# The last columns of v among the first products of the RWKV scan, and the gate's matmuls spread through each step

## The chip, the cores and the metric

The kernel runs on one core of a Trainium2 chip. The metric is the device time of one execution in microseconds (us). Of the kernel before there are three such times and one profiled execution. The engines are TensorE (PE in the profile, with its weight loads as PEld), VectorE (DVE), ScalarE (ACT), GpSimd (POOL), and SyncE (SP), whose queue issues most of the transfers.

## The reference, cut to what matters

Two layers over 1024 tokens of width 1024; the change is in the second, an RWKV-7 layer with a SiLU gate (16 heads of 64):

```python
def rwkv7_scan(r, w, k, v, kk, a):
    ...
    def step(state, inp):
        r_t, w_t, k_t, v_t, kk_t, a_t = inp
        sa = jnp.einsum('bhvk,bhk->bhv', state, -kk_t)
        state = (state * w_t[:, :, None, :]
                 + sa[..., None] * (kk_t * a_t)[:, :, None, :]
                 + v_t[..., None] * k_t[:, :, None, :])
        y_t = jnp.einsum('bhvk,bhk->bhv', state, r_t)
        return state, y_t

def odd_mixer(h, mu, w_r, w_k, w_v, w_g, w0, w1, w2, a0, a1, a2, k_k, k_a, r_k, lnx_w, lnx_b, w_o):
    ...
    xr, xw, xk, xv, xa, xg = [h + xx * mu[i] for i in range(6)]
    r = xr @ w_r
    k = xk @ w_k
    v = xv @ w_v
    g = xg @ w_g
    ...
    ys = rwkv7_scan(tm(rh), tm(wh), tm(kh), tm(vh), tm(kk), tm(ah)).transpose(1, 0, 2, 3)
    ...
    y = (y + bonus.reshape(B, S, D)).astype(h.dtype) * jax.nn.silu(g)
    return y @ w_o
```

The kernel doesn't run the scan token by token. It cuts the 1024 tokens into 16 chunks of 64 and works on them in 8 blocks of two chunks; within a chunk the recurrence becomes products of 64x64 matrices for each head, and a triangular matrix to invert for each head.

## The kernel before, in words

**Projections.** r, k, v and g are 1024x1024 projections. Each operand is split into a high and a low part, so a product takes three matmuls. `odd_layer` makes r, k and v in turn, 256 columns at a time (c = 0 to 3), and in two halves of the tokens (f = 0, 1: token blocks 0 to 3 and 4 to 7 of 128). For v, one 128-token group of 256 columns is 24 matmuls of 128x256; two groups share a PSUM tile, which `ev_v` evicts on ACT into a tile and stores to v_d in DRAM. The last piece of v (c = 3, f = 1) is 96 matmuls and ends right before the scan. The gate g isn't made in `odd_layer`: `Gate.pieces` makes it during the scan, 16 groups of 8 pieces, 3 matmuls of 128x512 in each piece (L943). After a group's last piece ACT evicts it through SiLU and stores it to sg_d.

**The scan.** Three strings of tokens set the order of all work of the scan: `SCAN_START`, `SCAN_STEP` (run six times, for blocks 0 to 5), `SCAN_END`. Each token calls a function of the same short name; every engine gets its instructions in that order, SP its transfers too. The tokens that matter here:
- `ld`: load A and BK of a chunk (0.5 MB each, L1001 and L1003); `uv`: load its v rows.
- `al` (`alphas`, 32 + 32 matmuls of 64x64 in the profile's count, L1043 and L1046): makes M and AK from A and BK; ACT evicts them. `sM` stores M of a block's two chunks to DRAM (MA, L1055, four transfers), `lM` loads it back in another layout (Nt, L1099).
- `ip`, `ia`, `ie`, `ib`: the inverse of the 32x32 diagonal blocks, on DVE, cut into rows that `ib` calls a few at a time; `ic` stores the result (XT, L1171) and `lX` loads it as X (L1179).
- `mx`, `ma` (L1197), `mb` (L1210): the remaining quarter of the inverse from X and M. `ma` is the first on PE to need X.
- `sc` (`scores`, L1030, one half of a chunk): needs A and BK; ACT evicts it to MY. `mA`, `mY`: POOL masks AK and MY.
- `dec` (`decayed`, L1062): POOL scales BK in place when al and sc have read it. `T` (`transposed`, L1072): PE transposes the scaled BK.
- `V` and `U` (L1225, L1250), `st` (L1275, the product for the next state, which DVE adds to it), `Y` (L1285), `W` (L1235 and, for the output of the chunk before, L1294): the recurrence proper. `keep`: POOL scales the state.
- `g` with a number: that many gate pieces; `L`, `wx`, `gl`, `gx`: load and split the gate's weights; `xl`: load the gate's x for the second token half.

In a step, U, st, Y and W work on the block's own chunks c and c+1; al, sc, dec, T and the start of the inverse work two blocks ahead, and ic, lX, mx, ma, mb one block ahead. The work around each step's X is thus: SP stores M (`sM`), loads A and BK, stores XT, loads Nt, loads X; PE goes on with U1 to W2 and gate pieces until ma.

All of SP's transfers go out in order: one that waits for its data holds those behind it.

Of the kernel before, what the change touches and what calls it, by code (L numbers as in the profile page):

```python
# [8 lines left out]
F32 = mybir.dt.float32  # L9
# [8 lines left out]
P = 128  # L18
KT = D // P
NB = S // P  # L20
CB = 256
# [28 lines left out]
EVEN_PLAN = (  # L50
    "q0 k0 h0 z2 h1 q1 h2 k1 h3 va0 s0 h4 u0 h5 z3 h6 z0 h7 va1 s1 u1 z1")
SCAN_START = (
# [4 lines left out]
SCAN_STEP = (  # L57
    "U0 al0 ib2 st0 al1 Y0 uv1 keep1 mA0 mA1 W1 sM0 sc0 ib3 ld6 U1 sc1 g1 mY0 mY1 ic0 st1 dec0 lM0 Y1 g1 W2 keep2 "
    "ip0 lX0 gx1 uv2 sc2 Yd0 T0 g1 sc3 ia0 ld7 mx0 ma0 dec1 ie0 g2 mb0 g2 T1 g2 ib3 gl2")
SCAN_END = (  # L60
# [82 lines left out]
def load_wm(g, w, c0):  # L143

    return wm(split_wm(g, [load_m(g, w, c0, i) for i in range(2)]))
# [576 lines left out]
def mixed(g, hT, i, fs, x):  # L722

    nc = g.nc
    xh, xl = x
    for f in fs:
        for kk in range(4):
            h = g.s4([P, 2, 512], F32R, "xh")
            l = g.s4([P, 2, 512], F32R, "xl")
            for j in range(2):  # L730
                k = 2 * kk + j
                t = g.s2([P, 512], F32, "xm")
                if j and i == 0:
                    nc.vector.tensor_scalar(t, hT[kk, f][:, j, 1:513], g.onemu[:, i, k:k + 1], None, op0=OP.mult)
                else:
                    nc.scalar.activation(t, hT[kk, f][:, j, 1:513], AF.Copy, scale=g.onemu[:, i, k:k + 1])  # L736
                nc.vector.scalar_tensor_tensor(t, hT[kk, f][:, j, 0:512], g.pr[:, i, k:k + 1], t,  # L737
                                               op0=OP.mult, op1=OP.add)
                nc.scalar.activation(h[:, j], t, AF.Copy)
                (nc.vector if j or not i else nc.gpsimd).tensor_tensor(l[:, j], t, h[:, j].bitcast(F32), OP.subtract)  # L740
            xh[kk, f], xl[kk, f] = h, l
# [89 lines left out]
            nc.sync.dma_start(g.BK_d[64:128, f * 8:(f + 1) * 8, p, 1 - j], BK[64:128, :, j])  # L831


def odd_layer(g, a, hT, wt, out):
    nc, tc = g.nc, g.tc
    st = ExitStack()
    pool = st.enter_context(tc.tile_pool(name="prep", bufs=1, reuse_waits="tile"))
    prep = Prep(g, a, pool)

    def store(dst, ps, func):  # L840
        t = g.s2([P, 512], F32, "rt")
        nc.scalar.activation(t, ps, func)
        nc.sync.dma_start(dst, t)

    def ev_r(c):
        return lambda m, f, ps: store(g.r_d[2 * c + m][:, f * 512:(f + 1) * 512], ps, AF.Copy)

    def ev_k(c):
        return lambda m, f, ps: prep(2 * c + m, f, ps)

    def ev_v(c):
        def fn(b2, ps):
            t = g.s2([P, 2, 2, CB // 2], F32, "rt")
            for j in range(2):
                nc.scalar.activation(t[:, j].rearrange("p e (q d) -> p e q d", d=CH),
                                     ps[:, j].rearrange("p (q e d) -> p e q d", e=2, d=CH), AF.Copy)
                nc.sync.dma_start(g.v_d[(2 * b2 + j) * P:(2 * b2 + j + 1) * P, :, c * P:(c + 1) * P], t[:, j])
        return fn

    plan = []  # L860
    for i, n, fn, ld, ev in ((0, "rw_wr", chan_major, load_wm, ev_r), (2, "rw_wk", chan_major, load_wm, ev_k),
                             (3, "rw_wv", token_major, load_wk, ev_v)):
        for c in range(D // CB):
            plan.append((i, a[n][0], fn, ld, ev, c))
    w = load_wm(g, plan[0][1], 0)
    xn = ({}, {})
    mixed(g, hT, 0, (0,), xn)
    lora(g, hT, wt, prep.TH, prep.UA)
    mixed(g, hT, 0, (1,), xn)
    for j, (i, W, fn, ld, ev, c) in enumerate(plan):  # L870
        if c == 0:
            x, xn = xn, ({}, {})
        if j + 1 < len(plan):
            nxt = plan[j + 1][3](g, plan[j + 1][1], plan[j + 1][5] * CB)
        else:
            gate = Gate(g, a["rw_wg"][0], xn)
            gate.load(0)
            gate.load(1)
            gate.split(0)
            gate.split(1)  # L880
        if j == 9:
            norms(g)
        if j == XD:
            mixed_out(g, hT, 5, 1, g.xg_d)
        if c == 3:
            ni = plan[j + 1][0] if j + 1 < len(plan) else 5
            fn(g, x, w, ev(c), (0,))
            mixed(g, hT, ni, (0,), xn)
            fn(g, x, w, ev(c), (1,))
            if ni != 5:  # L890
                mixed(g, hT, ni, (1,), xn)
        else:
            fn(g, x, w, ev(c))
        w = nxt
    st.close()
    g.p2s.close()
    late = st.enter_context(tc.tile_pool(name="scan", bufs=1, reuse_waits="tile"))
    gate.pool = late
    g.s2 = lambda shape, dtype, name: late.tile(shape, dtype, name=name, bufs=1)
    rw = Rwkv(g, late)  # L900
    for c in range(2):
        rw.load(c)
    o = Out(g, a, out, late)
    with tc.manual_schedule(engines=ENG | {mybir.EngineType.SP}):
        rw.start(gate)
        for b in range(NB - 2):
            rw.step(b, gate)
    with tc.manual_schedule(engines=ENG | {mybir.EngineType.SP}):
        rw.end(gate, o)
    st.close()  # L910
# [67 lines left out]
class Rwkv:  # L978
# [326 lines left out]
    def start(self, gate):  # L1305
        g, nc = self.g, self.g.nc

        def zs(i):
            nc.gpsimd.memset(self.new_S(0), 0.0)

        self.pm = g.bB([P, 2, 2, 4, CH], "pm")
        ops = dict(L=gate.load, wx=gate.split, xl=gate.load_x, ld=self.load,
                   g=lambda i: [next(gate.rest, None) for _ in range(i)],
                   sc=lambda i: self.scores(i // 2, i % 2), al=self.alphas, sM=self.store_M, lM=self.load_M,
                   ip=self.inverse_p, ia=self.inverse_a, ie=self.inverse_d, ib=lambda i: [next(self.rows, None) for _ in range(i)],
                   ic=self.inverse_c, lX=self.load_X, mx=self.merge_x, ma=self.merge_a, mb=self.merge_b,
                   dec=self.decayed, T=self.transposed, mA=self.mask_AK, mY=self.mask_MY,
                   uv=self.load_uv, V=lambda i: list(self.Wkeys(i)), W=self.W, keep=self.keep, zs=zs)
        for name, i in order(SCAN_START):
            ops[name](i)  # L1320
# [244 lines left out]
```

## Time and profile before

| what | us |
|---|---|
| three runs | 1478.01, 1482.53, 1484.24 |
| median | 1482.53 |
| profiled execution | 1480.0 |
| its span | 1478.1 |
| PE busy in the span | 1308.3 (89%) |
| DVE, ACT, POOL busy | 897.8, 627.8, 548.4 |

The mean granted clock of PE over the span is 0.941. The span holds the work of one execution; the execution's own time is 1.9 us longer. The page of the profile gives busy time for each engine, the chain of work that ended last, and groups of instructions by line; the trace behind it can be cut into windows of time and listed by instruction. In rows of waits the numbers are the total in us, the number of waits, the longest. In a timeline row the first number is the start, the second the duration, and a bracket at the end gives the idle time before it and what ended that. In a row of windows the stretch is followed by its length, the busy time and number of instructions of each engine, PE's granted clock (1.00 is full speed), the share of DMA and GB/s.

### The profile page before, as it was taken

What the parts mean: (1) busy time and instruction counts of PE and PEld (TensorE: products, weight loads), DVE (VectorE), ACT (ScalarE), POOL (GpSimd) and SP (SyncE); (2) the same over time, 40 slices, a digit from 0 to 9 for tenths busy, and PEclk for the clock granted to TensorE, in tenths of its full rate; (3) what the DMA queues carried; (4) which work ended last, traced back from release to release, by engine and by line L of the source; (5) the groups of instructions that cost most, each with busy time, mean ns of one, the idle gap of its engine ahead of it and who ended that gap; (6) DMA issues with size and microseconds to landing.
All of it is one profiled execution on the core that took longest, in us unless ns stands there. A gap on an engine that the chain in (4) does not pass through costs nothing.

```text
span 1478.1 us, 30910 instructions
## 1 busy us (share of the span) xinstructions
PE 1308.3 (89%) x12773; PEld 1108.9 (75%) x12773; DVE 897.8 (61%) x1489; ACT 627.8 (42%) x1188; POOL 548.4 (37%) x353
## 2 busy tenths in 40 slices
PE   5899999899997999999997868998978788887877
PEld 5887788778896799978864436896767666667877
DVE  8741535663557426771599888512856677768884
ACT  4421535552454323552545554323434344454322
POOL 8750102030112612221343353203644444387751
PEclk9999999899999999999999979998978898979998
DMA  6377435350443334224177547517586666676412
GB/s 221 86 259 196 114 128 158 83 131 15 137 121 101 124 119 143 74 74 140 43 220 203 125 103 204 143 48 207 142 244 162 154 168 167 187 212 228 143 36 93
DMA packets 253275, 209.15 MB, mean 141 GB/s; under 512 B 79648, under 2 KB 215424, under 8 KB 253136
## 3 DMA queue, kind: packets, MB, share of 16 engines
q1 hardware_dynamic: 249536, 198.27, 47.1%
q10 hardware_dynamic: 3600, 8.91, 1.8%
q8 instruction: 100, 1.64, 0.5%
q14 instruction: 39, 0.32, 0.1%
HBM read 135.71 MB, written 71.43 MB: 140 GB/s over the span
## 4 chain that ended last, share of the span: by engine, by line
PE 53%; DVE 17%; DMA 9%; issue 8%; ACT 6%; POOL 4%; SPq 2%; ACTq 0%; DVEq 0%; POOLq 0%
PE pj L153 33%; PE pj L943 4%; PE pt L572 2%; PE pj L1477 2%; DMA kl<-dk 1%; DMA BK<-BK_d 1%; DMA w<-in_rw_a_dram 1%; DMA XT<-xm 1%; PE sp L562 1%; PE sp L559 1%; PE op L580 1%; DMA X<-XT 1%; ACT wh L105 1%; PE py L1285 1%; DVE xm L737 1%
## 5 line engine op out<-in xcount | busy, mean ns | idle before, releaser
L106 POOL TENSOR_TENSOR wl<-wraw,wh 128x1024 fp32r<-128x1024 f32 x38 | 93.6, 2466 | 168.6 <-ACT wh L105 157.5
L106 DVE TENSOR_TENSOR wl<-wraw,wh 128x1024 fp32r<-128x1024 f32 x46 | 70.8, 1545 | 94.5 <-ACT wh L105 51.4
L153 PE MATMUL pj<-hh,wh 128*128 128x512 f32 x320 | 127.3, 398 | 0.0
L153 PE MATMUL pj<-hh,wl 128*128 128x512 f32 x320 | 126.6, 396 | 0.0
L153 PE MATMUL pj<-hl,wh 128*128 128x512 f32 x320 | 126.6, 396 | 0.0
L105 ACT ACTIVATE wh<-wraw 128x1024 fp32r<-128x1024 f32 x84 | 88.1, 1056 | 61.9 <-DMA wraw<-in_w_in_even_dram 25.1
L153 PE MATMUL pj<-xl,wh 128*128 128x512 f32 x256 | 102.3, 400 | 2.6 <-DVE xl L740 2.6
L153 PE MATMUL pj<-xh,wh 128*128 128x512 f32 x256 | 102.2, 401 | 2.4 <-ACT ks L789 2.4
L153 PE MATMUL pj<-xh,wl 128*128 128x512 f32 x256 | 101.8, 398 | 0.2 <-POOL wl L106 0.2
L566 DVE CUSTOM_DVE_ANT_0 sc<-sp,tb 128x128 f32<-128x128 f32 (+3 forms) x64 | 48.2, 753 | 59.4 <-PE sp L562 50.8
L1477 PE MATMUL pj<-wh,yh 128*128 128x256 f32 x256 | 75.4, 294 | 5.1 <-DVE x L1481 3.9
L1477 PE MATMUL pj<-wh,yl 128*128 128x256 f32 x256 | 74.4, 291 | 4.6 <-POOL yl L106 4.5
L153 PE MATMUL pj<-wh,hh 128*128 128x256 f32 x256 | 75.1, 296 | 3.2 <-ACT hh L265 2.9
L737 DVE SCALAR_TENSOR_TENSOR xm<-hT,pr,xm 128x512 f32<-128x512 f32 x56 | 50.0, 933 | 44.0 <-ACT xm L736 43.7
L153 PE MATMUL pj<-wh,hl 128*128 128x256 f32 x256 | 75.3, 295 | 1.2 <-DVE hl L266 1.2
L153 PE MATMUL pj<-wh,yl 128*128 128x256 f32 x256 | 73.7, 288 | 1.9 <-POOL yl L624 1.9
L153 PE MATMUL pj<-wl,hh 128*128 128x256 f32 x256 | 74.6, 292 | 0.0
L153 PE MATMUL pj<-wh,yh 128*128 128x256 f32 x256 | 73.3, 286 | 0.8 <-ACT yh L623 0.8
L1477 PE MATMUL pj<-wl,yh 128*128 128x256 f32 x256 | 74.0, 289 | 0.0
L153 PE MATMUL pj<-wl,yh 128*128 128x256 f32 x256 | 72.9, 285 | 0.0
L153 PE MATMUL pj<-wh,xh 128*128 128x256 f32 x256 | 72.2, 282 | 0.6 <-ACT ks L789 0.5
L153 PE MATMUL pj<-wl,xh 128*128 128x256 f32 x256 | 72.2, 282 | 0.0
(320 smaller groups left out, 4062.3 us busy)
## 6 DMA issues: line engine op xcount, KB each, us to landing
wraw<-in_w_in_even_dram SPq DMA_DIRECT2D x28, 512.0 KB
tb<-tb SPq DMA_DIRECT2D x16, 512.0 KB
A_d<-AR SPq DMA_DIRECT2D x16, 512.0 KB
wraw<-in_rw_wg_dram SPq DMA_DIRECT2D x16, 512.0 KB
A<-A_d SPq DMA_DIRECT2D x16, 512.0 KB
BK<-BK_d SPq DMA_DIRECT2D x16, 512.0 KB
xt<-in_x_dram SPq DMA_DIRECT2D x8, 512.0 KB
dv<-vt SPq DMA_DIRECT2D x16, 256.0 KB
```

Source lines behind the costliest of these rows:

```text
L105: nc.scalar.activation(hi, raw, AF.Copy)
L106: sub.tensor_tensor(lo, raw, hi.bitcast(F32), OP.subtract)
L153: nc.tensor.matmul(ps, a(k), b(k), start=(n == 0), stop=(n == 3 * KT - 1))
L559: nc.tensor.matmul(sp[:, c0:c1], qs[:, b * P:(b + 1) * P], kh[:, c0:c1], start=True, stop=False)
L562: nc.tensor.matmul(sp[:, c0:c1], qs[:, b * P:(b + 1) * P], kl[:, c0:c1], start=False, stop=True)
L566: nc.vector.tensor_tensor_reduce(sc[:, :n], sp[:, :n], tb[:, off:off + n], 1.0, BIG, OP.add, OP.min, mn)
L572: nc.tensor.transpose(pt[:, j - j0, :], sc[:, j * P:(j + 1) * P], g.ident)
L580: nc.tensor.matmul(op[:, s0:QW], vt[:, j, :], pth[j // 4][:, j % 4, s0:QW], start=(j == 0), stop=False)
L737: nc.vector.scalar_tensor_tensor(t, hT[kk, f][:, j, 0:512], g.pr[:, i, k:k + 1], t, op0=OP.mult, op1=OP.add)
L943: nc.tensor.matmul(ps, u[:, k], v[:, k % 2], start=(k == 0 and i == 0), stop=(k == KT - 1 and i == 2))
L1285: nc.tensor.matmul(self.py[64 - 64 * e:128 - 64 * e, q], t["MY"][:, 8 * e + q], t["UV"][:, e, q], start=q == 0, stop=False)
L1477: nc.tensor.matmul(ps[:, i, :], u[:, k], v[:, k % 4], start=(k == 0 and j == 0), stop=(k == KT - 1 and j == 2))
```

## The change

Three things.

First, the last half of v's last columns is no longer made ahead of the scan. For the last projection `odd_layer` makes a generator, `last_values`, with the same 96 matmuls in 8 steps of 12 matmuls each, and the new token `vp` takes that many steps of it. `ev_v` takes its tile under the name XT, which the scan's pool shares with the gate's eviction.

Second, `SCAN_START` is ordered anew: al0 and al1 of the first block come behind 36 and 48 matmuls of the v half, with no gate piece ahead of them (15 before); the rest of v follows, then Nt's load, then the inverse and the gate pieces. Ahead of ma0 there are 32 gate pieces (58 before); the number of pieces in `SCAN_START` is the same, 64.

Third, `SCAN_STEP` has the same nine pieces, but six ahead of ma0 and three behind it (three and six before), each between two groups of the recurrence. al1 moves from between st0 and Y0 to behind W1, sc0 to behind Y1, sc1 with dec0 to behind W2, and T0 stands directly behind them. `SCAN_END` is unchanged.

```diff
 SCAN_START = (
-    "g4 L2 g4 L4 L3 g7 al0 al1 sM0 ip0 wx2 g2 sc0 L7 g2 sc1 dec0 L9 uv0 ld2 g3 wx3 sc2 g2 wx4 sc3 dec1 g2 lM0 T0 "
-    "ld3 L6 g4 mA0 mY0 ia0 L5 g2 al2 wx5 g2 sc4 T1 ld4 g3 al3 sM1 ie0 sc5 dec2 g3 wx6 ib8 sc6 g2 sc7 dec3 uv1 T2 "
-    "zs0 g3 ic0 g4 wx7 mA1 mY1 ip1 lM1 lX0 keep0 g4 T3 g5 L8 mx0 xl0 V0 uv2 ma0 g2 wx8 xl1 ia1 mA2 g2 xl2 mb0 ie1 "
-    "W0 ld5 mA3 g2 xl3 ib3")
+    "vp3 al0 vp1 al1 sM0 ip0 vp2 lM0 vp2 ia0 ie0 g4 L2 sc0 g4 L4 L3 sc1 dec0 ib8 ld2 g7 wx2 g2 sc2 L7 g2 sc3 dec1 "
+    "L9 uv0 T0 ld3 g3 wx3 ic0 ip1 lX0 g2 wx4 T1 al2 mA0 mY0 g2 L6 ld4 g4 sc4 L5 g2 wx5 mx0 al3 sM1 V0 uv2 ma0 sc5 "
+    "dec2 g2 mb0 T2 g3 lM1 sc6 g3 wx6 sc7 dec3 ia1 mA1 mY1 uv1 g2 zs0 g3 ie1 T3 g4 wx7 keep0 g4 mA2 g5 L8 xl0 g2 "
+    "wx8 xl1 g2 xl2 W0 ld5 mA3 g2 xl3 ib3")
 SCAN_STEP = (
-    "U0 al0 ib2 st0 al1 Y0 uv1 keep1 mA0 mA1 W1 sM0 sc0 ib3 ld6 U1 sc1 g1 mY0 mY1 ic0 st1 dec0 lM0 Y1 g1 W2 keep2 "
-    "ip0 lX0 gx1 uv2 sc2 Yd0 T0 g1 sc3 ia0 ld7 mx0 ma0 dec1 ie0 g2 mb0 g2 T1 g2 ib3 gl2")
+    "U0 al0 g1 ib2 st0 Y0 uv1 keep1 g1 W1 al1 mA0 mA1 sM0 ib3 ld6 U1 g1 gx1 g1 mY0 mY1 ic0 st1 lM0 Y1 sc0 g1 W2 "
+    "sc1 dec0 keep2 ip0 lX0 uv2 T0 Yd0 g1 sc2 sc3 ia0 ld7 mx0 ma0 dec1 ie0 g2 mb0 T1 g1 ib3 gl2")
...
+def last_values(g, x, w, evac):
+
+    wh, wl = w
+    for b in range(4, 8):
+        sl = slice((b % 4) * P, (b % 4 + 1) * P)
+        if b % 2 == 0:
+            ps = g.bA([P, 2, CB], "pj")
+        n = 0
+        for k in range(KT):
+            for i, v in ((0, wh), (0, wl), (1, wh)):
+                g.nc.tensor.matmul(ps[:, b % 2, :], x[i][k // 2, 1][:, k % 2, sl], v(k), start=(n == 0), stop=(n == 3 * KT - 1))
+                n += 1
+            if k == 3:
+                yield
+        if b % 2:
+            evac(b // 2, ps)
+        yield
...
     def ev_v(c):
         def fn(b2, ps):
-            t = g.s2([P, 2, 2, CB // 2], F32, "rt")
+            t = g.s2([P, 512], F32, "XT").rearrange("p (j e c) -> p j e c", j=2, e=2)
...
             mixed(g, hT, ni, (0,), xn)
-            fn(g, x, w, ev(c), (1,))
             if ni != 5:
+                fn(g, x, w, ev(c), (1,))
                 mixed(g, hT, ni, (1,), xn)
+            else:
+                gate.last = last_values(g, x, w, ev(c))
...
-        ops = dict(L=gate.load, wx=gate.split, xl=gate.load_x, ld=self.load,
+        ops = dict(vp=lambda i: [next(gate.last, None) for _ in range(i)], L=gate.load, wx=gate.split, xl=gate.load_x, ld=self.load,
```

The lines of the code below line 850 move down by 19 to 21 (L943 becomes L964, L1043 L1064, L1197 L1218).

On PE, at the scan's beginning, the matmuls of the gate (L943, tiles pj, xh, xl, wh, wl) that stood ahead of al0 (L1043 and L1046) before:

```order
L943 MATMUL pj<-xh,wh 128x512
L943 MATMUL pj<-xl,wh 128x512
L943 MATMUL pj<-xh,wl 128x512
L1043 MATMUL pt<-BK,A 64x64 x2
L1046 MATMUL pt<-A,BK 64x64 x2
```

The same place now, with v's last half (L844) ahead of al0 (L1064, L1067):

```order
L844 MATMUL pj<-wh,xh 128x256
L844 MATMUL pj<-wl,xh 128x256
L844 MATMUL pj<-wh,xl 128x256
L1064 MATMUL pt<-BK,A 64x64 x2
L1067 MATMUL pt<-A,BK 64x64 x2
```

al0 stood behind all of v and 45 gate matmuls; now it stands behind 36 of the 96 matmuls of v's last half.

On SP, at the same place, the order of transfers from the last stores of v (v_d) to the first load of Nt, before (wraw is the gate's weights):

```order
L857 DMA v_d<-rt 256x1x128 x18
L1001 DMA A<-A_d 128x1024 x2
L928 DMA wraw<-in_rw_wg_dram 128x8x128
L857 DMA v_d<-rt 256x1x128 x2
L928 DMA wraw<-in_rw_wg_dram 128x8x128 x2
L1003 DMA BK<-BK_d 128x1024 x2
L1055 DMA MA_129<-M 32x16x32 x4
L928 DMA wraw<-in_rw_wg_dram 128x8x128 x2
L1013 DMA UV<-v_d 64x512 x2
L1001 DMA A<-A_d 128x1024
L1003 DMA BK<-BK_d 128x1024
L1099 DMA Nt<-MA_129 64x1024 x2
```

And now:

```order
L876 DMA v_d<-XT 256x1x128 x16
L1022 DMA A<-A_d 128x1024 x2
L1024 DMA BK<-BK_d 128x1024 x2
L876 DMA v_d<-XT 256x1x128 x2
L1076 DMA MA_129<-M 32x16x32 x4
L1120 DMA Nt<-MA_129 64x1024 x2
L876 DMA v_d<-XT 256x1x128 x2
L949 DMA wraw<-in_rw_wg_dram 128x8x128 x3
```

BK's loads follow A's directly, and Nt's load follows the store of MA directly; the loads of the gate's weights and of the next chunks come behind both.

On PE, in a step, from the end of W2 (L1235, L1294) to ma (L1197), before:

```order
L1235 MATMUL ch<-S,A 64x64 x2
L1294 MATMUL py<-S,A 64x64 x2
L1030 MATMUL pm<-A,BK 64x64 x16
L1072 MATMUL pt<-ident,BK 128x128 x8
L943 MATMUL pj<-xh,wh 128x512
L943 MATMUL pj<-xl,wh 128x512
L943 MATMUL pj<-xh,wl 128x512
L1030 MATMUL pm<-A,BK 64x64 x16
L1197 MATMUL pt<-X,M 32x32 x32
```

And now (W2 L1256 and L1315, sc L1051, T0 L1093, the gate L964, ma L1218):

```order
L1256 MATMUL ch<-S,A 64x64 x2
L1315 MATMUL py<-S,A 64x64 x2
L1051 MATMUL pm<-A,BK 64x64 x16
L1093 MATMUL pt<-ident,BK 128x128 x8
L964 MATMUL pj<-xh,wh 128x512
L964 MATMUL pj<-xl,wh 128x512
L964 MATMUL pj<-xh,wl 128x512
L1051 MATMUL pm<-A,BK 64x64 x32
L1218 MATMUL pt<-X,M 32x32 x32
```

Here the first sc is sc2 before and sc1 now: T0 transposes BK after POOL's scaling, which waits for sc1; sc1 stood further up, behind U1, and stands now directly ahead of T0.

## The prediction

> **What bounds the kernel now.** I read the chain of work that ended last first, then windows cut at the borders of the scan (its beginning, its six steps, its end; the first window is the last half of v's projection), then what TensorE (PE) waits for in the steps.
>
> ```profile
> PE 53%; DVE 17%; DMA 9%; issue 8%; ACT 6%; POOL 4%; SPq 2%; ACTq 0%; DVEq 0%; POOLq 0%
> ```
>
> ```profile
> core 0: us, PE busy (x) PEld busy (x) DVE busy (x) ACT busy (x) POOL busy (x), PEclk, DMA share, GB/s
> 991.50:1003.10 11.60, 11.60 (x100) 11.60 (x99) 9.79 (x10) 9.86 (x19) 6.04 (x4) 1.00 0.14 38
> 1003.10:1088.90 85.80, 71.90 (x929) 56.20 (x927) 38.57 (x57) 29.54 (x47) 38.36 (x33) 0.88 0.72 202
> 1088.90:1127.30 38.40, 32.50 (x812) 27.38 (x811) 28.14 (x49) 15.33 (x27) 16.00 (x15) 0.78 0.73 207
> 1127.30:1160.50 33.20, 27.21 (x812) 22.88 (x811) 21.77 (x38) 15.00 (x27) 15.78 (x15) 0.90 0.65 167
> 1160.50:1192.40 31.90, 26.92 (x812) 22.83 (x811) 19.66 (x35) 15.29 (x27) 15.86 (x15) 0.95 0.60 150
> 1192.40:1225.70 33.30, 27.10 (x812) 22.39 (x811) 22.65 (x39) 14.73 (x26) 15.96 (x15) 0.95 0.68 170
> 1225.70:1259.80 34.10, 27.84 (x812) 23.29 (x811) 24.46 (x43) 14.74 (x26) 15.78 (x15) 0.90 0.65 166
> 1259.80:1292.70 32.90, 27.54 (x805) 22.54 (x804) 22.04 (x40) 13.63 (x24) 13.89 (x14) 0.90 0.66 171
> 1292.70:1478.10 185.40, 145.81 (x1671) 136.74 (x1670) 134.95 (x175) 69.58 (x146) 114.80 (x51) 0.88 0.43 143
> ```
>
> ```profile
> PE pt L1197 <- DMA X<-XT: 10.4, 7, 3.3
> PE pm L1030 <- issue: 6.7, 5, 2.7
> PE pt L1072 <- POOL BK L1062: 2.5, 3, 1.8
> PE pt L1043 <- DMA BK<-BK_d: 2.4, 1, 2.4
> ```
>
> PE is the largest part of the chain, but not all of it. The v half runs without a gap: 11.60 us for 96 matmuls of v and the first of the gate, some 0.12 us each. The scan's beginning leaves PE idle for 85.8 - 71.9 = 13.9 us, and each step for 5 to 6 us, both at a granted clock below 1. So time can be won in two ways: less idle PE, and fewer windows at half clock. In the steps the largest wait is that of ma (line 1197) for the transfer X, the next is the sequencer's own ("issue") ahead of sc (line 1030).
>
> **The beginning before.** The chain of waits over this stretch, and PE's and SP's timelines:
>
> ```profile
> 1003.14 5.58 PE pj L943 x24
> 1009.33 6.83 DMA BK<-BK_d
> 1021.07 0.61 ACT M L1047
> 1029.05 9.04 DMA Nt<-MA
> 1074.59 3.63 DMA X<-XT
> ```
>
> ```profile
> 1016.21 0.27 PE L1043 MATMUL pt<-BK,A 64*64 64x64 f32 x2 [2.64 <-DMA BK<-BK_d]
> ...
> 1076.18 0.28 PE L1197 MATMUL pt<-X,M 32*32 32x32 f32 x2 [6.32 <-DMA X<-XT]
> 1078.27 1.91 PE L1197 MATMUL pt<-X,M 32*32 32x32 f32 x62 [1.80 <-DMA X<-XT]
> ```
>
> ```profile
> 1021.69 1.96 SPq L1055 DMA_DIRECT2D MA<-M  x4
> ...
> 1028.55 1.09 SPq L1099 DMA_DIRECT2D Nt<-MA  x2
> ```
>
> ```profile
> 1038.10:1069.20 31.10, 30.68 (x392) 24.39 (x392) 29.91 (x34) 13.49 (x23) 22.48 (x15) 1.00 0.48 133
> 1083.70:1104.10 20.40, 17.35 (x553) 15.17 (x553) 18.74 (x36) 7.88 (x14) 6.31 (x6) 0.81 0.70 242
> ```
>
> One path: BK lands 1016.2, al0 and al1 make M, SP stores it (1021.69) and issues the load of Nt only 6.86 us later, behind six other loads; Nt lands 1038.1; DVE inverts (31.1 us); X lands 1078.27, 9.1 us after the inverse. PE fills that time with gate pieces and runs out: 6.32 + 1.80 = 8.1 us of waiting, then half clock (ma takes 1.91 us).
>
> **The change at the beginning.** In the chain 24 gate matmuls follow each other in 5.58 us, so a piece (three of them) takes 0.70 us in a run. al0 and al1 now come behind the first half of v and 36 of the last 96 matmuls of v, without a gate piece ahead of them.
> - BK: A and BK (two chunks, 2 MB) are now issued right behind the stores of v's first half, not at 1009.3. That half ends at 991.5, its stores some 2 us later; al0 needs 1.5 MB, 6 us at the 258 GB/s of the window 1184.6 to 1192.4 below: BK lands near 1000 (an estimate). PE finishes its 36 matmuls at 991.5 + 4.3 = 995.8 and waits about 4 us (2.6 before); then half clock, two al of 1.9 us (ma's ratio, 1.19 to 1.91, below) with 12 matmuls of v between: al1 done near 1006.5, 14.7 us before 1021.2.
> - Nt: SP has the load directly behind the store. M's eviction 0.6, store 2, landing some 3 us: Nt lands near 1015, against 1038.1, so 23 us earlier.
> - The inverse: 31.1 us in one place and 20.4 us in the other, where POOL is busy for 22.48 and 6.31 us beside it. POOL's splits and scalings lie beside it again, thinner; I take 25 (bounds 20.4 and 31.1): done 1040, X at 1040 + 9.1 = 1049.
> - PE until ma0: from 1006.5 the last 48 matmuls of v (5.6), 32 gate pieces (22.4), five sc (0.7 each, 3.5), two al (2.2), two T (2.1) and V0 (1.1) make 36.9: PE arrives at 1043.5 and waits 5.5 us (8.1 before), then about 3 us lost to half clock.
> - After ma0: ma 1.2, three sc 2.1, 32 pieces 22.4, mb 1.2, two T 2.1, W0 1.1, together 30.1, and 1.5 us of small waits: U0 at 1049 + 30.1 + 3 + 1.5 = 1083.6, against 1088.9. **Term: -5** us. With the inverse at 20.4 X comes with PE, and the half clock goes too: -12; at 31.1 X lands at 1055: +1.
>
> [...]
>
> **The change in a step.** Windows from Y0's end to X's landing and from X to the step's end, at half and at full clock; then PE's timeline (durations of what moves, ma after longer and shorter waits), SP's and POOL's:
>
> ```profile
> 1133.10:1150.40 17.30, 11.62 (x405) 9.60 (x403) 9.49 (x14) 7.63 (x14) 14.46 (x15) 0.97 0.68 157
> 1150.40:1160.50 10.10, 10.09 (x152) 8.18 (x152) 9.51 (x22) 4.01 (x7) 0.00 (x0) 0.71 0.89 255
> ...
> 1184.60:1192.40 7.80, 7.80 (x162) 6.35 (x154) 7.41 (x16) 4.64 (x8) 1.91 (x1) 1.00 0.93 258
> ```
>
> ```profile
> 1130.89 0.27 PE L1043 MATMUL pt<-BK,A 64*64 64x64 f32 x2
> ...
> 1132.00 1.15 PE L1285 MATMUL py<-UV,MY 128*64 128x64 f32 x32
> ...
> 1150.41 1.91 PE L1197 MATMUL pt<-X,M 32*32 32x32 f32 x62 [0.30 <-DMA X<-XT]
> ...
> 1170.89 0.69 PE L1030 MATMUL pm<-A,BK 64*64 64x64 f32 x32
> 1171.51 0.50 PE L943 MATMUL pj<-xh,wh 128*128 128x512 f32 x1
> ...
> 1172.40 0.69 PE L1275 MATMUL ch<-UV,BKT 128*64 128x64 f32 x16
> ...
> 1181.07 1.97 PE L1072 MATMUL pt<-ident,BK 128*128 128x128 f32 x8
> ...
> 1216.55 1.19 PE L1197 MATMUL pt<-X,M 32*32 32x32 f32 x62 [0.83 <-DMA X<-XT]
> ```
>
> ```profile
> 1135.07 2.17 SPq L1055 DMA_DIRECT2D MA<-M  x4
> ```
>
> ```profile
> 1142.20 1.91 POOL L1062 TENSOR_TENSOR BK<-BK,EC 128x1024 f32<-128x1024 f32 x1
> ```
>
> al1's matmuls run from 1130.89 to 1132.00 (1.1 us), Y0's 1.15; U, W, st and Y have as many and get 1.1 to 1.15 each. sc takes 0.69; a lone piece 0.9 (1171.51 to 1172.40), two 1.6; T half of the 1.97 at half clock, 1.0.
>
> X stands on SP behind the store of MA, the loads of A and BK, and Nt, so it lands a fixed time after MA's issue: 1150.41 - 1135.07 = 15.3 us in step 1. MA was issued 7.75 us after the step's start (1127.3). Now al1 comes behind W1: U0 1.15, al0 1.1, piece 0.9, st0 1.15, Y0 1.15, piece 0.9, W1 1.15, al1 1.1 make 8.6; with the eviction and SP's issue MA goes out at 9.35, **1.6 us later**, and X lands at 24.65 (9.35 + 15.3). PE reaches ma at: 8.6 + U1 1.15, two pieces 1.6, st1 1.15, Y1 1.15, sc0 0.7, piece 0.9, W2 1.15, sc1 0.7 = 17.1; T0 stands straight behind and waits for POOL's 1.91 us scaling (to about 19.2; 2.5 us in all steps together before); T0 1.0, piece 0.9, two sc 1.4: 22.5. So PE waits some 2.1 us at ma, and T0's wait is hidden under it. If X came earlier, T0's 2 us would stand open. The issue waits (6.7 us) fall into the same slack.
>
> Behind X stand three pieces fewer: 7.8 - 2.1 = 5.7 us at full clock, 10.1 - 2.1 = 8.0 at half. A step is 30.4 or 32.7, against a mean of 33.1 over steps 1 to 5. Which clock? A wait of 0.83 us left ma at 1.19; the longest X wait (3.3 in the list, step 1) was followed by a ma of 1.91, the longest issue wait ahead of sc (2.7) by the T of 1.97. 2.1 is nearer to the latter, so I take 31.8 between the two, a gain of 1.3. Bounds: -2.7 (full clock) and +0.8 (X as late in its step as in step 3, 1216.55 - 1192.4 = 24.15, plus 1.6, then 8.0: 33.8). **Term: five steps, -6.5** (-13.5 to +4).
>
> [...]
>
> Step 0 took 38.4 at clock 0.78 with a 2.4 us wait for BK (line 1043). That load is now issued with more lead; at 33.4, as the slower steps before, **-5** (0 if load and clock stay, -7 like the others). The end (185.4) is left alone: 0.
>
> **Sum.** 1480.0 (span 1478.1) - 5 - 5 - 6.5 = 1463.5; the median shown, 1482.53, lies 2.5 above that execution: **1466 us**.
>
> **Rivals.**
> - Slower: al1 now stands behind W1, and W1 reads the state that DVE adds between its rows of the inverse. Any wait there delays al1, MA and, through SP's order, X one for one. Price: a wait of 1.5 us gives 25.8 + 1.5 + 8.0 = 35.3, +2.2 in each of five steps, +11, and step 0 no faster; with -5 at the beginning 1488, with 0 there 1493: I give 1490. It decides from a wait of about 1 us. Against: the list above has no wait for DVE among the largest, and between st0 and W1 PE has Y0 and a piece, 2.05 us of cover, against al1 and Y0, 2.25, before. Chance 0.13.
> - Only the beginning gains (X binds the steps; BK's wait goes): -5 - 2.4: 1475. 0.17.
> - Only the steps gain, the inverse being long: +1 - 5 - 6.5: 1472. 0.14.
> - Full clock in the steps: a wait near 2 us, between the 0.83 that kept it and the 2.7 that lost it, is too short to lower it. -5 - 5 - 13.5: 1459; with a short inverse 1452. 0.18. [...]
> - The change doesn't do what it says: SP's queue is held by v's last stores, Nt lands no earlier in effect, waits change places: 1482. 0.06.
>
> The forecast has 0.32. **Range 1453 to 1488**: from the best of the beginning and steps nearly together (1480.0 + 2.5 - 12 - 5 - 13 = 1452.5) to the worst terms (+1, 0, +4: 1487.5). Half a per cent, 7.4 us, is about what a measurement of this kernel can tell from no change: the bound of "faster" is 1475.1. Faster 0.66: the forecast, the third and fourth rivals and half of the second, which stands on the bound, are 0.725, less 0.065 for sums of these that end above it; same 0.20: those two remainders and the last rival; slower 0.14: the first, and 0.01 of the last.
>
> **What would show it.** Right: al0 near 1000 after a wait of some 4 us; Nt landing before 1017; X of block 0 before 1052, with a wait under 6 us at ma0; no BK wait in step 0; MA issued 9 to 9.5 us after U0, X 24 to 25; T0 waiting 2 us in every step, steps of 31 to 32.5 us. Wrong: U0 after 1088, W1 waiting for DVE, steps over 33.1 us, or an end stage that differs from 185.4 by more than 2 us.

## The result, and the profile after

The change makes the kernel slower: 1497.33 us in the median of 6 runs (1490.38 to 1500.84), against 1479.83 in 6 runs of the kernel before, the three above among them. The medians differ by 17.5 us; the ratio on record is 1.0129, 95% interval 1.0099 to 1.0159, some 19 us, and the experiments below are compared by such ratios. The forecast was 1466, with a range of 1453 to 1488. The profiled execution took 1494.9 us (span 1492.8).

The stages of the changed kernel's profile, cut at the same places as those of before: v's first 36 matmuls of the last half (from the end of its first half at 988.4), the scan's beginning up to U0, the six steps, the end. The columns are as before.

```profile
988.40:992.80 4.40, 4.40 (x38) 4.23 (x36) 2.83 (x5) 4.13 (x8) 0.00 (x0) 1.00 0.47 93
992.80:1090.90 98.10, 77.61 (x993) 63.10 (x992) 42.05 (x67) 35.62 (x59) 43.88 (x36) 0.90 0.56 162
1090.90:1126.20 35.30, 26.65 (x812) 21.70 (x811) 21.03 (x38) 15.84 (x27) 16.01 (x15) 0.95 0.85 256
1126.20:1163.90 37.70, 28.55 (x813) 23.07 (x813) 27.91 (x44) 15.18 (x27) 16.70 (x15) 0.89 0.60 159
1163.90:1199.70 35.80, 29.95 (x814) 24.84 (x813) 23.30 (x39) 15.29 (x26) 16.47 (x15) 0.83 0.59 149
1199.70:1233.10 33.40, 26.90 (x816) 21.80 (x815) 19.23 (x35) 14.95 (x26) 16.20 (x15) 0.95 0.62 159
1233.10:1263.00 29.90, 24.89 (x812) 20.58 (x811) 21.25 (x38) 15.14 (x26) 16.88 (x15) 1.00 0.64 162
1263.00:1307.60 44.60, 32.47 (x804) 25.81 (x803) 26.05 (x45) 14.24 (x25) 14.01 (x14) 0.75 0.66 182
1307.60:1492.80 185.20, 142.24 (x1671) 133.81 (x1670) 133.27 (x175) 69.64 (x146) 114.76 (x51) 0.89 0.40 133
```

From the end of v's first half to U0 it takes 4.4 + 98.1 = 102.5 us; before it was 11.6 + 85.8 = 97.4. So the beginning lost 5.1 us where 5 were to be won. The six steps take 216.7 against 203.8, 12.9 more, and 11.7 of these stand in the last (44.6 against 32.9, at a clock of 0.75). The end is the same (185.2, 185.4). What PE waits for in the beginning (first fence) and in the steps (second):

```profile
PE pt L1218 <- ACT M L1068: 7.3, 1, 7.3
PE pt L1064 <- DMA BK<-BK_d: 4.3, 1, 4.3
PE ch L1246 <- POOL AK L1099: 3.3, 1, 3.3
```

```profile
PE pt L1093 <- POOL BK L1083: 13.8, 6, 2.7
PE pm L1051 <- ACT MY L1052: 6.7, 7, 2.4
PE pj L964 <- ACT wh L105: 5.6, 1, 5.6
PE ch L1246 <- issue: 3.2, 2, 1.9
```

X, the largest wait before, is in neither list. In its place stand waits for ACT and POOL: ma0 (L1218) 7.3 us for ACT, T (L1093) 2 us in each step for POOL's scaling, sc (L1051) for ACT's eviction, and one gate piece (L964) 5.6 us for the split of its weights. The waits put down to the sequencer ("issue") are as large as before in the steps, some 14 us together.

**The 7.3 us at ma0.** The timelines of PE, ACT, SP and DVE there:

```profile
1055.35 0.85 PE L1218 MATMUL pt<-X,M 32*32 32x32 f32 x24 [7.34 <-ACT M L1068]
```

```profile
1053.76 1.06 ACT L105 ACTIVATE wh<-wraw 128x1024 fp32r<-128x1024 f32 x1 [11.22 <-DMA wraw<-in_rw_wg_dram]
1054.72 0.58 ACT L1068 ACTIVATE M<-pt 128x512 f32<-128x512 f32 x1
1055.20 0.59 ACT L1069 ACTIVATE AK<-pt 128x512 f32<-128x512 f32 x1
```

```profile
1041.45 2.30 SPq L1200 DMA_DIRECT2D X<-XT  x4
...
1045.70 0.42 SPq L949 DMA_DIRECT2D wraw<-in_rw_wg_dram  x1
```

```profile
1013.61 0.42 DVE L1142 TENSOR_TENSOR DN<-Nt,rn 128x256 f32<-128x256 f32 x1 [11.44 <-DMA Nt<-MA]
...
1044.82 0.71 DVE L1206 STREAM_TRANSPOSE rt<-X 128x512 f32<-128x512 f32 x1 [7.01 <-DMA X<-XT]
```

X is there at 1044.82, when DVE reads it. ma0 starts at 1055.35, directly after ACT has evicted the M that the profile names. That M is al3's, of the next block: ACT stood 11.22 us before its split of a gate weight (wx5) that waited for the load, and M's eviction is behind it in ACT's order. The load (L5) was issued at 1045.70, behind X's on SP, which had waited 2.3 us for XT to land. al3 and ma0 take their PSUM from one pair of buffers in the code (`bC`, bufs=2), so ma0 can't start before al3's is evicted: that eviction ends at 1055.30. The data path of the forecast came in time; a weight load that it never counted didn't. PE itself came to ma0 at 1048.0 (1055.35 - 7.34), behind X and not ahead of it, since V0 had waited 3.3 us for POOL's mask of AK.

**The 5.6 us in the last step.** ACT and PE there:

```profile
1275.47 0.60 ACT L970 ACTIVATE XT<-pj 128x512 f32<-128x512 f32 x1
...
1279.24 0.33 ACTq L971 DMA_DIRECT2D sg_d<-XT  x1
1279.67 1.06 ACT L105 ACTIVATE wh<-wraw 128x1024 fp32r<-128x1024 f32 x1 [3.60 <-DMA XT<-xm]
```

```profile
1280.78 0.80 PE L964 MATMUL pj<-xh,wh 128*128 128x512 f32 x1 [5.61 <-ACT wh L105]
```

The piece needs the next weights at once: the group before ends with the piece ahead of `gx1`, and the split of the next weights stands directly between. Nine pieces a step against eight in a group move that border by one piece in each step; in the last it falls on gx1's new place. And ACT isn't free: the store of the finished group (sg_d) waits 3.6 us, with ACT behind it, for a transfer on SP, the inverse's store XT, on which its data doesn't depend. In the third and fifth steps the store holds ACT too, for 1.72 us (until X lands) and 2.25 us (until a load of A lands).

### The profile page after: what moved, and what is told of

It is laid out like the page before. It is cut to its first block, busy times and chain, and to the rows that moved or that the text cites. A ratio compares the mean times of both kernels' runs of the same rounds, so it can differ in the third digit from the quotient of the medians.

```text
span 1492.8 us, 30914 instructions
## 1 busy us (share of the span) xinstructions
PE 1298.1 (87%) x12773; PEld 1097.4 (74%) x12773; DVE 888.6 (60%) x1489; ACT 630.5 (42%) x1188; POOL 554.0 (37%) x353
## 4 chain that ended last, share of the span: by engine, by line
PE 51%; DVE 15%; DMA 9%; issue 8%; POOL 8%; ACT 7%; SPq 2%; ACTq 0%; DVEq 0%; POOLq 0%
PE pj L153 31%; PE pj L964 4%; POOL MY L1105 2%; PE pj L1498 2%; PE pj L711 1%; PE pt L572 1%; DMA wraw<-in_w_in_even_dram 1%; DMA BK<-BK_d 1%; PE pt L1093 1%; PE op L580 1%; ACT wh L105 1%; PE sp L559 1%; POOL BK L1083 1%; PE sp L562 1%; POOL wl L106 1%
## 5 line engine op out<-in xcount | busy, mean ns | idle before, releaser
L106 POOL TENSOR_TENSOR wl<-wraw,wh 128x1024 fp32r<-128x1024 f32 x38 | 94.3, 2483 | 161.3 <-ACT wh L105 148.5
L106 DVE TENSOR_TENSOR wl<-wraw,wh 128x1024 fp32r<-128x1024 f32 x46 | 72.7, 1587 | 95.5 <-ACT wh L105 50.1
L575 DVE TENSOR_TENSOR ptl<-pt,pth 128x512 fp32r<-128x512 f32 (+2 forms) x96 | 52.3, 553 | 29.8 <-ACT pth L574 16.7
L153 PEld LDWEIGHTS pj<-hh,wl 128*128 128x128 f32 x320 | 60.1, 188 | 13.3
```

The costliest lines, as they stand in the source:

```text
L106: sub.tensor_tensor(lo, raw, hi.bitcast(F32), OP.subtract)
L153: nc.tensor.matmul(ps, a(k), b(k), start=(n == 0), stop=(n == 3 * KT - 1))
L575: nc.vector.tensor_tensor(ptl[j0 // 4][:, 0:j1 - j0, i * P:(i + 1) * P], pt[:, :j1 - j0, :], o.bitcast(F32), OP.subtract)
```

## The experiments

Ratios are to runs of the kernel before, with 95% intervals. A step's or an end's length is that of the one profiled execution.

**The two halves of the change.** First the old step with the new beginning, then the new step with the old beginning.

```diff
-SCAN_STEP = (new)
+SCAN_STEP = (as before)
```

> The changed kernel with the old SCAN_STEP: only v's last columns and the order of the scan's beginning are changed. In the profile of the change the beginning (from v's first half to U0) is 5.1 us longer than before and the six steps 12.9 us. If the two parts add up, this kernel is some 5 us slower than before (about 1485). Rival: the beginning's loss comes out of what the new steps ask of it; then it gains the 5 us that the prediction gave it (about 1475).

1.0092 (1.0064 to 1.012): some 14 us slower, neither of the two numbers expected. The profile has the same wait at ma0 (7.9 us for ACT), so the loss there isn't asked for by the new steps. It also has a first step of 43.3 us (38.4 before), with 5.1 us of waiting for BK.

```diff
-SCAN_STEP = (as before)
+SCAN_STEP = (new)
```

> The kernel before with the new SCAN_STEP alone. If the parts add up: 13 us slower than before (about 1493), with a wait of some 5 us for the gate's split weights (ACT wh) in the sixth step and T waiting 2 us for POOL in each step. Rival: the steps lose only because the new beginning leaves buffers and loads late; then within 3 us of before.

1.0081 (1.0056 to 1.0106): 12 us slower, with a wait of 6.4 us for ACT wh in the sixth step. Each half costs time by itself. Together (1.0129) they seem to cost less than their sum (1.0173), though the intervals don't part the two; both spoil the same last step (40.1 us with the new beginning alone, 42.4 with the new step alone, 44.6 with both). With the new beginning alone the steps are those of before in every token, but ACT is held in the last one by the gate's store, now for 8.79 us, and with it the eviction of ma's result (rt), which PE's mb needs; mb starts at 1298.24, at the end of that eviction, after 7.9 us of waiting (the profile puts it down to a DVE operation that ended then too):

```profile
1287.71 0.63 ACT L970 ACTIVATE XT<-pj 128x512 f32<-128x512 f32 x1
1296.76 0.33 ACTq L971 DMA_DIRECT2D sg_d<-XT  x1
1297.13 0.60 ACT L1052 ACTIVATE MY<-pm 128x512 f32<-128x512 f32 x1 [8.79 <-DMA lnw<-in_rw_lnw_dram]
```

lnw is a load of norm weights and has nothing to do with the gate. In the kernel before the same store waits for the store of Y (2.97 us). The program's list of instructions, with the semaphores that they wait on, names the link: in this program each transfer of SP and ACT counts on one of eight completion semaphores (DMAHW0 to 7), and the store waits on the transfer that had its semaphore last. The traces agree: the 757 transfers of SP and ACT in the change count on eight semaphores, and the store of the last step is issued at 1279.24, 0.08 us after the last completion of XT's store, which has its semaphore (1279.16); in the kernel before at 1283.56, 0.08 us after that of Y's (1283.48). Here are the 14th gate store and a transfer on SP of the same semaphore, in the change, in the new beginning alone, and in the kernel before:

```
L971 DMA sg_d<-XT 128x512 [waits DMAHW6_49,Activation_49]
L1192 DMA XT_143<-xm 1024x1x32 [waits DMAHW6_49,DVE_49,Pool_49]

L971 DMA sg_d<-XT 128x512 [waits DMAHW3_49,Activation_49]
L1400 DMA lnw<-in_rw_lnw_dram 128x1024 [waits DMAHW3_49]

L950 DMA sg_d<-XT 128x512 [waits DMAHW1_49,Activation_49]
L1302 DMA Y_150<-Y 64x2x512 [waits DMAHW1_49]
```

**The weights' split.** gx1 earlier in the step, in two places.

```diff
-    "U0 al0 g1 ib2 st0 ... U1 g1 gx1 g1 mY0
+    "U0 al0 gx1 g1 ib2 st0 ... U1 g2 mY0
```

> The changed kernel with the split of the gate's weights (gx1) at the step's first place, behind al0, and not directly ahead of the gate piece that may need it. Theory: in the sixth step that piece waits 5.6 us for ACT, which is held by the store of the group before, and half the clock is lost behind it, some 3 us; all of it goes, so 8 to 9 us faster than the change (about 1488). Rival (the POOL wait of T0 and the late al1 set the steps): the sixth step only gives the wait to X or T, at most 2 us faster.

1.0234 (1.0199 to 1.0268), some 15 us slower than the change: neither theory's number. The last step falls to 34.5 us, as the theory has it, but the third to fifth take 41.0, 36.2 and 37.7 (35.8, 33.4 and 29.9 in the change). Waits of PE over these three, and DVE in the third:

```profile
PE ch L1256 <- DVE S L1298: 10.2, 3, 4.0
```

```profile
1168.80 1.23 DVE L106 TENSOR_TENSOR wl<-wraw,wh 128x1024 fp32r<-128x1024 f32 x1 [5.57 <-ACT wh L105]
...
1173.44 0.68 DVE L1298 TENSOR_TENSOR S<-ch,S 128x512 f32<-128x512 f32 x1
```

The low half of the split (L106) runs on DVE, now ahead of the addition of the state (L1298), and DVE waits 5.6 us for the high half from ACT; W1 (L1256) waits for the state. This is the wait that the prediction's slower rival named, which in the change's own steps didn't occur. So the split goes behind Y0, when DVE has added the state:

```diff
-    "... Y0 uv1 keep1 g1 W1 al1 mA0 mA1 sM0 ib3 ld6 U1 g1 gx1 g1 mY0
+    "... Y0 uv1 keep1 gx1 g1 W1 al1 mA0 mA1 sM0 ib3 ld6 U1 g2 mY0
```

> The changed kernel with gx1 behind Y0 and nothing else: two gate pieces, W1, al1 and U1 then stand between the split and the piece that may need it, and DVE adds the state first. Theory: the 5.6 us wait for ACT wh in the sixth step and the half clock behind it go, and W1 waits for DVE no more than before: 6 to 9 us faster than the change (about 1489). Rival: as with gx1 ahead of st0, some engine ahead of W1 gets late: no gain or slower.

1490.49 us, 1.0076 (1.0049 to 1.0102): 0.5% under the change's ratio, 8 us, in the middle of what was expected; the two intervals just touch. The wait for wh is gone. The last step and the end, in the profile:

```profile
1269.90:1302.40 32.50, 25.53 (x805) 20.73 (x804) 23.47 (x40) 13.55 (x24) 14.94 (x14) 0.95 0.71 189
1302.40:1491.90 189.50, 144.93 (x1671) 135.25 (x1670) 137.46 (x180) 70.01 (x147) 114.72 (x51) 0.89 0.42 139
```

The last step is 12.1 us shorter than in the change, but the end is 4.3 longer, so 7.8 are won over both, which is what the runs have. Why the end grows wasn't followed; some of DVE's work moves into it (26.1 us busy in the step and 133.3 in the end before the edit, 23.5 and 137.5 with it). The wait of T for POOL is as large as ever (13.3 us over the steps), so it isn't that wait which cost these 8 us.

**The weights' load.** L6 and L5 ahead of the first inverse's store.

```diff
-... T0 ld3 g3 wx3 ic0 ip1 lX0 g2 wx4 T1 al2 mA0 mY0 g2 L6 ld4 g4 sc4 L5 g2 wx5 mx0 al3
+... T0 ld3 L6 L5 g3 wx3 ic0 ip1 lX0 g2 wx4 T1 al2 mA0 mY0 g2 ld4 g4 sc4 g2 wx5 mx0 al3
```

> The changed kernel with the loads of two gate weights (L6, L5) ahead of the store of the first inverse (ic0) and no longer behind lX0. Theory: in the beginning ACT waits 11 us for that load (its split wx5 stands ahead of the eviction of M of al3), and ma0 waits 7.3 us for ACT although X is there; with the load some 8 us earlier ma0 starts within 2 us of PE's arrival: 5 to 8 us faster than the change (about 1490). Rival: ma0 waits for X or V0 for POOL in its place, at most 2 us faster.

1490.51 us, 1.0078 (1.0052 to 1.0104): 7 to 8 us, with intervals that just touch again. PE, at V0 and ma0:

```profile
1047.62 1.98 PE L1246 MATMUL ch<-UV,AK 64*64 64x64 f32 x32 [3.41 <-POOL AK L1099]
1049.52 1.92 PE L1218 MATMUL pt<-X,M 32*32 32x32 f32 x64
```

ma0 follows V0 without a wait, and from the end of v's first half to U0 it takes 96.8 us (102.5 in the change). The first step takes 38.3, though (35.3 in the change). What is left is V0's wait, for POOL's mask of AK, which stands behind a memset that waits for XT's store (9.29 us in the change, whose memset starts at 1041.53). With the masks ahead of that too:

```diff
-... L6 L5 g3 wx3 ic0 ip1 lX0 g2 wx4 T1 al2 mA0 mY0 g2
+... L6 L5 g3 wx3 mA0 mY0 ic0 ip1 lX0 g2 wx4 T1 al2 g2
```

> The changed kernel with L6 and L5 ahead of ic0 and, in the beginning, POOL's masks of AK and MY (mA0, mY0) ahead of ic0 and ip1, whose memset waits for the first inverse's store. Theory: V0's wait for AK (3.4 us with L5 early) goes and ma0 takes at most 2 us of it as a wait for X: 1 to 3 us faster than the kernel with L5 alone (about 1488). Rival: PE only waits at ma0 in its place, no gain.

1.0104 (1.0081 to 1.0127): no gain; the interval overlaps that with L5 alone, and that of the change. PE at ma0:

```profile
1048.52 0.21 PE L1218 MATMUL pt<-X,M 32*32 32x32 f32 x2 [1.38 <-DMA X<-XT]
1049.45 1.19 PE L1218 MATMUL pt<-X,M 32*32 32x32 f32 x62 [0.71 <-DMA X<-XT]
```

As the rival had it: V0's 3.4 us go, and ma0 waits 2.1 us for X. From there to U0 the profile has 39.6 us at a granted clock of 0.87, against 35.5 at 0.93 with L5 alone.

**The two causes together**, gx1 behind Y0 and L6/L5 ahead of ic0 (the edits above):

> The changed kernel with gx1 behind Y0 and L6 and L5 ahead of ic0: the two named causes alone. Theory: 7 us from the loads (as measured) and 6 to 9 from gx1: 1481 to 1485, within 0.5% of before. Rival: T0's wait for POOL and the stores on ACT cost as much again: 1488 or more.

1481.61 us, 1.0024 (0.9999 to 1.0048), an interval well apart from the change's: of the 19 us, 15 to 16 are these two, and they add up. What either is worth by itself (some 8 us) is less sure, by the intervals above.

**T0.** A piece and sc2 between sc1 and T0.

```diff
-... lX0 uv2 T0 Yd0 g1 sc2 sc3 ia0
+... lX0 uv2 Yd0 g1 sc2 T0 sc3 ia0
```

> The changed kernel with T0 behind sc2, so that a gate piece and sc2 (1.65 us) stand between sc1 and T0, and T0 between sc2 and sc3. T0's wait for POOL (13.8 us over the six steps) falls below 1 us each and sc3's wait for MY (6.7) goes. If PE's own order sets the steps, 10 to 16 us faster than the change (about 1484). Rival: X takes the place of both (it lands some 24 us after U0, where PE then arrives at 24 to 25): at most 5 us faster.

1.0118 (1.0091 to 1.0145), the same as the change within the intervals. T's wait fell from 13.8 to 1.8 us, but sc's for MY rose to 11.6 and X's came back with 4.7: the rival's gain of at most 5 us, with MY more than X in T's place. T's wait stood in front of others and cost little.

**The gate's stores on POOL**, whose transfers have semaphores of their own in the program's list (DMASW0 to 7), in the change and, as a control, in the kernel before:

```diff
-        g.nc.scalar.dma_start(g.sg_d[n % KT, :, f * 512:(f + 1) * 512], t)
+        g.nc.gpsimd.dma_start(g.sg_d[n % KT, :, f * 512:(f + 1) * 512], t)
```

> The changed kernel with the gate's stores (sg_d) issued by POOL and not by ACT. Theory: the store's issue waits on ACT for an earlier transfer with which it shares a completion semaphore (XT in the sixth step 3.6 us, X in the third 1.7 us), and ACT's splits and evictions behind it hold PE (5.6 and 2.4 us, and half clock behind them). On POOL the stores have semaphores of their own, so 8 to 12 us faster than the change (about 1487). Rival: ACT isn't what holds PE there, or POOL becomes late by the issue: no gain or slower.

1.0091 (1.0057 to 1.0126), 5 us or so below the change, but the intervals overlap. The last step and the end:

```profile
1263.80:1299.00 35.20, 27.05 (x804) 21.97 (x803) 21.98 (x39) 13.43 (x25) 15.36 (x15) 0.90 0.65 171
1299.00:1491.80 192.80, 146.72 (x1671) 137.87 (x1670) 143.33 (x181) 70.05 (x147) 114.67 (x53) 0.86 0.41 135
```

The last step loses 9.4 us and the end gains 7.6, so in this profile most of it comes back there.

> The kernel before with the gate's stores issued by POOL: a control. In its sixth step ACT is held 3.0 us by the same store, without a large wait of PE behind it. Theory: within 4 us of before, so the hold costs the change and not the kernel before. Rival: as much faster as the change gets (8 us or more).

1.0001 (0.9979 to 1.0022), as the theory had it. The end is 193.9 us here too, behind a last step of 26.9. Then L6/L5 earlier, T0 late and the stores on POOL, in the change:

> The changed kernel with the three edits together: L6 and L5 earlier, the gate's stores on POOL, T0 between sc2 and sc3. If the three waits are what the change lost, they take back 7 + 9 + 5 us: 1476 or below, level with before or faster, with U0 of the first step some 5 us ahead of the change and steps of 30 to 33 us. Rival: further waits follow (BK's load, X, issue): 1485 or more.

1.0064 (1.0038 to 1.0089), 1486.76 us, as the rival had it: lower than each alone (1.0078, 1.0118, 1.0091), though its interval is apart only from that of T0 alone, and not level with before. X is back as the largest wait in the steps:

```profile
PE pt L1218 <- DMA X<-XT: 9.3, 7, 2.9
PE pt L1093 <- POOL BK L1083: 4.8, 6, 1.7
```

**All of them, and the step alone.** The stores on POOL for the first 14 groups only; the last two fall into the end, and were thought to be what made it longer:

```diff
+        (g.nc.gpsimd if n < 14 else g.nc.scalar).dma_start(g.sg_d[n % KT, ...
```

The change with L6/L5 and the masks earlier, T0 late, gx1 behind Y0, and these stores:

> The changed kernel with five edits: L6/L5 and the masks earlier in the beginning, T0 between sc2 and sc3, gx1 behind Y0 (so that DVE adds the state before it splits the weights), and the gate's stores on POOL for its first 14 groups, on ACT for the last two. If order alone made the change slow, all its new waits are gone but X's: U0 some 3 us ahead of before, steps of 31 to 32.5 us, the end at 185: 1468 to 1474, faster than before. Rival: X, which waited behind the others, binds the steps at 33 to 34 us: within 4 us of before (1478).

1477.98 us, 0.9996 (0.9979 to 1.0013): level with before, as the rival had it. X waits 10.7 us in its steps. The kernel before with these stores and nothing else:

> The kernel before with the gate's stores on POOL for the first 14 groups and on ACT for the last two. With all 16 on POOL the profile has steps 1 to 2 us shorter in sum and an end 8 us longer; with the last two on ACT the end is as before (185.4), so 1 to 5 us faster than before (about 1475). Rival: the end's 8 us aren't from the stores; then no difference.

1474.12 us, 0.9966 (0.9946 to 0.9986): faster than both kernels, as expected, but not for the reason expected. The end is 189.8 us and not 185.4; kernels with all stores on ACT can have such an end too (189.5 above, 192.7 in the last kernel of this section). The kernel before with these stores and the mended new step:

> The kernel before with the new SCAN_STEP in which T0 stands between sc2 and sc3 and gx1 behind Y0, and with the stores as in e11. It shows what the spread of the gate's pieces is worth without the waits it brought. Theory of the prediction (X 1.6 us later, three pieces fewer behind it): steps of 31.5 to 32.5, 5 to 8 us faster than e11. Rival: X late and half clock: steps of 33 to 34, no gain over e11.

1474.0 us, 0.9966 (0.9947 to 0.9985): no gain over the stores alone, as the rival had it. It differs from the kernel with five edits (1477.98) only in the beginning, which is the old one here: the new beginning, mended, gains nothing either and is rather 4 us slower, though the intervals overlap. And the mended step with the stores on ACT:

> The kernel before with the new SCAN_STEP, gx1 behind Y0 and T0 between sc2 and sc3, the stores on ACT as before. If the spread of the pieces gives nothing because X is waited for in each step as before: within 3 us of before (1478). If the stores on POOL were what made e12 faster: 4 us above e12. If the spread is worth what was forecast: 1470 or below.

1480.17 us, 1.0011 (0.9995 to 1.0027). The last two kernels differ in nothing but the stores, and their intervals don't touch. PE's waits in the six steps, first with the stores on ACT, then on POOL:

```profile
PE pm L1030 <- ACT MY L1031: 12.1, 7, 5.6
PE pt L1197 <- DMA X<-XT: 4.5, 5, 2.0
```

```profile
PE pt L1197 <- DMA X<-XT: 9.4, 8, 2.7
PE pt L1072 <- POOL BK L1062: 3.6, 6, 1.3
```

With the stores on ACT sc waits 12.1 us for evictions; without, X takes its place. With the gate's pieces spread or not, the kernel takes the same time: 1474.0 and 1474.12 us with the stores on POOL, 1.0011 against before with them on ACT.

## Why the prediction was wrong

- **al0, Nt, the inverse, X: right.** al0 began at 997.17 after a wait of 4.3 us (8.8 us after the end of v's first half; 8.5 forecast, wait 4). Nt was there at 1013.61 (before 1017 forecast), the inverse took 24.2 us (25 taken), X was there by 1044.82 (1049 forecast, 3.1 less for the earlier end of v's first half). One term in it was luck: the forecast's parts for Nt (M's eviction 0.6, the store 2, landing 3) add up to 1012.1 and not to the 1015 written. From the issue of MA's store (1004.20) to Nt it took 9.4 us, where the store and the landing had 5. The window of the inverse shows POOL busy for 9.83 us, where the longer one of before had 22.48:

```profile
1013.60:1037.80 24.20, 21.63 (x245) 17.04 (x245) 23.05 (x34) 10.95 (x16) 9.83 (x4) 1.00 0.78 237
```

- **"PE arrives at 1043.5 and waits 5.5 us", the term -5: wrong, +5.1.** The step that failed is the list of what ma0 needs. It had PE's work and X, and not what stands ahead of PE's PSUM on ACT: wx5, its load L5, and SP's place behind X. The new string put L5 behind lX0, and lX0 waits for the inverse. The forecast followed SP's order for A, BK, MA and Nt, but not for the gate's weights. PE's own way was short too: it came at 1048.0 where 1040.4 was forecast (1043.5 less 3.1), with 3.3 us at V0 for POOL's mask, which has no term. Early loads take 7 to 8 us back, alone and on top of the mended split (by the ratios; some 4 with the masks moved too). The rest of the -5 isn't there either: with L5 and the masks mended the profile has 96.3 us from v's first half to U0 (9.2 to al0, 87.1 from there) against 97.4, 1.1 us.
- **Step 0, -5: right in sign, -3.1** (35.3 against 38.4); BK's wait fell from 2.4 to 0.9 us. It isn't that wait that made it: with L5 early BK's wait is 0.3 us and the step takes 38.3 again, with 5.7 us of "issue" waits in it (3.0 in the change).
- **"Five steps, -6.5": wrong, +16** (181.4 against 165.4). The term missed gx1: the string moved the split from behind lX0 to the place between U1's two pieces, and in the last step the second of them is the first to use the new weights. 8 us by the run with gx1 behind Y0. It also missed that ACT is held by the gate's store, in three of the steps (1.7, 2.3 and 3.6 us). MA's part was right: it went out 9.0 to 10.3 us after U0 in these steps (9.35 forecast).
- **"T0's wait is hidden under X's": right in effect, for another reason.** T waited the 2.1 to 2.7 us forecast in each step, and taking that away changed the time by nothing that the intervals can tell. But X didn't bind in the change; PE came to ma later than X, at 23.5 us after U0 in the step that was held up least (29.9 us long), at 26.7 to 28.2 in the three before it and at 36.5 in the last, where 22.5 was forecast, with "issue", MY and half clock on the way. "The issue waits fall into the same slack" failed with it: there was no slack.
- **The clock after 2.1 us: both.** T after the same 2.14 us wait, in the second and in the fifth step:

```profile
1149.08 1.97 PE L1093 MATMUL pt<-ident,BK 128*128 128x128 f32 x8 [2.14 <-POOL BK L1083]
...
1252.73 1.09 PE L1093 MATMUL pt<-ident,BK 128*128 128x128 f32 x8 [2.14 <-POOL BK L1083]
```

Half clock in one, full clock in the other, so no length of a wait between 0.83 and 2.7 us divides them. In this profile where it lies does: the granted clock changes only on a grid of 3.41 us (53 of its 54 stretches at one clock, all but the last, are whole multiples of it). Here are two neighbours on that grid around each of the two waits:

```profile
1145.62:1149.03 3.41, 1.32 (x92) 1.18 (x83) 0.00 (x0) 1.57 (x3) 1.92 (x2) 1.00 0.72 173
1149.03:1152.44 3.41, 3.36 (x19) 2.62 (x22) 1.84 (x8) 1.19 (x2) 1.99 (x4) 0.50 0.74 161
1248.02:1251.43 3.41, 2.58 (x109) 1.98 (x99) 0.81 (x2) 1.87 (x4) 3.02 (x3) 1.00 1.15 282
1251.43:1254.84 3.41, 2.11 (x35) 1.70 (x39) 0.14 (x1) 1.39 (x3) 3.25 (x5) 1.00 0.81 182
```

The first wait lies whole in one window, which has PE busy for 1.32 of 3.41 us (39%), and the next window runs at half clock. The second is divided by the border at 1251.43, both windows have PE busy for over 60%, and the clock stays. Over the whole profile 25 of the 27 windows from which the clock fell had PE busy for at most 45%, the other two for 55 and 60%; no window that kept it was under 46%. So a wait shorter than one window of the grid (2.14 us against 3.41) can stand ahead of half clock here.
- **The end, 0: right** (185.2), but with luck in it: it takes 188 to 193 us in all the changed kernels whose last step got shorter than 38 us.
- **The slower rival** had the right sign and the wrong mechanism: W1 waited for DVE's state in the steps only where gx1 was moved ahead of st0. What made the change slower wasn't among the rivals.
- **Without its two mishaps** the change is level with before (1.0024), not 1% faster; and with X waited for again in the mended steps, the rival "only the beginning gains" overrates even that: neither half gains, the beginning by the two kernels that differ in it alone (1477.98 and 1474.0), the step by those with it and without (1474.0 and 1474.12).

## What to carry to other kernels

When an order is rewritten, follow every token that moves relative to its consumer, the small ones above all: a load or a split that had slack at its old place can stand directly ahead of its first use in one pass of a loop, though not in the others. Ask of each engine's queue what holds the instruction that frees a PSUM buffer, not only what makes the data. A store that a compute engine issues can be a wait on that engine, for a transfer that has nothing to do with it (8.79 us on ACT for lnw, with the new beginning alone); try it on an engine that nothing waits for, and measure (here 14 of 16 stores moved gained 0.34%, all 16 nothing). And judge a stage together with the next: a last step shorter by 12 us was worth 8.

## What the runs showed that I had not expected

- A store issued by ACT waited 2.97, 3.60 and 8.79 us for transfers with which, by the program's list, it shares only a completion semaphore, and held ACT's evictions behind it. Which transfer that is changed with an edit far ahead. With 14 of the 16 on POOL the kernel before gains 0.34% (0.14 to 0.54). Why all 16 on POOL gain nothing (1.0001) wasn't followed further.
- Profiles of kernels with the same code up to al0 reach it between 992.7 (gx1 ahead of st0) and 1001.3 us (gx1 behind Y0). So stages are compared by their length, not by their place, and one profile's span tells little about 0.5%.
- The "issue" waits of PE go with the transfers of an instruction queue (q8: 100 of 16 KB in the change). In the trace of the change, each of the nine in the six steps (0.2 to 2.3 us) ends 1.3 to 1.7 us behind the end of a 16 KB transfer of an instruction queue, and so does each of the sixteen before (1.2 to 1.7 us); there are 38 such transfers in the steps of either kernel. The forecast had put these waits into the slack at ma, and their sum didn't change.
